# Retention stage of a two-block network on one core: state space steps over all head pairs, gate projection between token tiles, group norm and decays on GpSimd and ScalarE, one masked query product

## The chip, the cores and the metric

One core of a Trainium2 chip runs the whole program. The metric is device microseconds of one execution; the median of three runs before the change is 2362.76 us (2358.35 to 2370.51).

## The reference, cut to what matters

A first block (norm, input projection, retention beside a state space branch, mixing output, cross attention) is followed by a second one (two attentions and experts). The change touches retention and what shares its stage. All arrays have 1024 tokens; there are 8 heads with 64 columns for queries and keys and 128 for values, and chunks of 128 tokens:

```
proj = h @ w_in; q, k, v, g_ret, u, g_s5 = split(proj)
scores = einsum('bnihd,bnjhd->bnhij', qc, kc) * decay
inner  = einsum('bnhij,bnjhe->bnihe', scores, vc)
kv     = einsum('bnjhd,jh,bnjhe->bnhde', kc, k_w, vc)
R_next = chunk_decay * R + kv                    # a scan over the chunks
cross  = einsum('bnihd,ih,bnhde->bnihe', qc, q_w, R)
o   = (o - mean(o)) * rsqrt(var(o) + 1e-6)       # per head of 128 columns
ret = o * gn_g * silu(g_ret)
ssm = s5_branch(u) * silu(g_s5)
x   = x + concat([ret, ssm]) @ w_out
```

## The kernel before, in words

Products of float32 arrays run as three products of a high and a low part (`mm3`, lines 172 to 180). `weights` (L157) fetches a block of 1024 x 256 weights in two halves of 512 KB through one staging buffer `wraw`, casts each half to `whi` on ScalarE (L154) and subtracts on VectorE into `wlo` (L155); two such blocks fit at a time. All loads and stores named here are issued by SyncE, in one queue. The kernel writes instructions in program order, and a list scheduler then orders them for each engine: the earliest in program order that is ready goes first, so that later work fills gaps. On the chip each engine runs its own list strictly in order.

`retention` (L321) goes over four head pairs. For each pair it projects queries and keys of eight token tiles into the PSUM banks `m` (two of them), rotates them on VectorE (L356 to L360), and projects values (L367 to L371). Then comes a loop over four pairs of token tiles `m` (L437). `turn` (L377) transposes queries and keys of a tile on TensorE, copies the keys (`kT`, L384), multiplies the queries of each head by their decay into its half of a block-diagonal tile `qbd` (two VectorE instructions, L388) and once more into `qs` (L392), and scales the keys for the state (`kd`, two VectorE instructions, L397). `score` (L401) multiplies `kT` with `qbd` (L404) and `kd` with the values (L406), applies the mask (`st`, L408), and advances the state `rbd` with one VectorE instruction a head (L415, L417), since only its diagonal blocks hold anything. `output` (L420) multiplies `qs` with the state (256 columns, L422) and `st` with the values of each head (128 columns, L424). Between them `project` (L440) makes the retention gate. Group norm takes statistics of four heads (L463, L464), then an inverse root by a bit guess and two correction steps on VectorE (`rsqrt`, L182 to L198, tiles `rs_a` and `rs_y`), scales four times (L470) and multiplies by the gate (L472). `finish` (L426) transposes the result (L430) and stores it (L434, L435) in `ret_scr`; it is called one round later, as `late`.

`s5` (L594), the state space branch, is a generator of 32 steps: for each of 16 quads of groups, `phases` (angles, seven GpSimd instructions), `matrices` and `scan`, and for each two quads a `batch` that loads coefficients. `retention` yields the number of steps that are to be written next: two after every two token tiles of the query and value projections, none in the loop over `m`, so that in program order all 32 stand within the first two head pairs.

Behind retention, `mix_out` (L761) reads `ret_scr` back in eight blocks (`load_split`, L754: a load to `ls_raw`, which has two buffers, a cast to `r_hi`, a subtraction to `r_lo`; both tiles take memory that retention gives back). Next in program order is `h_last`, which is `s5_project` (L575) for the gate of the state space branch: four blocks of weights, each for four products of 24 matmuls of 512 columns, with a Silu on ScalarE (L588) and a 512 KB store for every two (L590). The first mixing product with `w_out` (L777 to L781) follows and reads all eight blocks of `ret` for every tile.

```
for steps in self.retention(h, rope, rc, rk, ret_scr):   # L1897
    for _ in range(steps):
        next(s5, None)
for _ in s5:
    pass
...
h2 = self.mix_out(hp, bp, lambda pj: self.s5_project(h, pj, g_scr, 4096, AF.Silu), ...)   # L1912
```

Of the kernel before, what the change touches and what calls it, by code (L numbers as in the profile page):

```python
# [20 lines left out]
P = 128  # L21
S = 1024
# [65 lines left out]
def lay_out(inputs):  # L88
    """The arrays of the launch: the inputs, those vectors that go along the partitions as columns, and the constants."""
# [30 lines left out]
class Net:  # L120
# [51 lines left out]
    def mm3(self, ps, lhs, rhs, ks, start=True, stop=True):  # L172
        """ps (+)= sum_k lhs_k^T rhs_k with both operands as exact float32r pairs; lhs, rhs: k -> (hi, lo)."""
# [39 lines left out]
    def normalise(self, xs, lo, n0):  # L213
        """Tiles xs [P tokens, D] in place to x / rms(x); the columns of the tiles from n0 in lo serve as scratch."""
# [9 lines left out]
    def gain(self, name):  # L224
        """A vector with features on the partitions, [P, k]."""
# [7 lines left out]
    def grow(self, name, pool, width=D):  # L233
        """A gain vector on every partition."""
# [6 lines left out]
    def to_feature(self, xs, hi, lo, n0, g):  # L241
        """Transpose the token tiles xs (each [P, D]) into columns n0*P.. of hi, lo [P, KD, tokens], times the gain g."""
# [11 lines left out]
    # ---------------------------------------------------------------- first norm  # L254
# [32 lines left out]
    def sincos(self, a, q, sin, cos):  # L287
        """sin and cos of the angles a, which (as q) is overwritten."""
# [10 lines left out]
    def exp_small(self, pool, x, name):  # L299
        """exp(x) to float32 accuracy on a small tile [p, n]."""  # L300
# [19 lines left out]
    # ---------------------------------------------------------------- retention  # L320
    def retention(self, h, rope, rc, rk, ret_scr):  # L321
        """Emits the retention branch, a step at a time."""
# [6 lines left out]
        qbd = [rc.tile([P, 2, P], F32, name=f"qbd{i}") for i in range(2)]  # L329
        rbd = [rc.tile([P, 2, P], F32, name=f"rbd{i}") for i in range(2)]  # L330
        for tl in qbd + rbd:
# [6 lines left out]
        for p in range(PAIRS):  # L338
            qw = rk.tile([P, P], F32, name="qw", tag="qw")
            nc.sync.dma_start(qw, t["k_ret_qw"][:, p * P:(p + 1) * P])  # L340
# [4 lines left out]
            for n in range(NT):  # L345
# [16 lines left out]
                if n % 2:  # L362
                    yield 2
            wv = self.weights([w[:, 1024 + p * 256:1024 + (p + 1) * 256]])
            vs = []
            for n in range(NT):
# [5 lines left out]
                if n % 2:  # L372
                    yield 2
# [3 lines left out]
            def turn(n):  # L377
                """Transposed queries (per head, with their decay) and keys of a token tile."""
# [6 lines left out]
                qb = qbd[n % 2]  # L385
                for h in range(2):
                    r = slice(h * 64, h * 64 + 64)
                    nc.vector.tensor_tensor(qb[r, h], ps[r, 0], qw[r], op=OP.mult)  # L388
                qs = None
                if n:  # L390
                    qs = rk.tile([P, P], F32, name="qs", tag="qs")
                    nc.vector.tensor_tensor(qs, ps[:, 0], qw, op=OP.mult)  # L392
                kd = None
                if n < NT - 1:
                    kd = rk.tile([P, 2, 64], F32, name="kd", tag="kd")
                    for h in range(2):
                        nc.vector.tensor_scalar(kd[:, h], qf[:, P + h * 64:P + h * 64 + 64], kw[:, 2 * p + h:2 * p + h + 1], None,  # L397
                                                op0=OP.mult)
                return kT, qb, qs, kd

            def score(n, kT, qb, kd):  # L401
                """Masked scores of a token tile and its term of the state."""
# [8 lines left out]
                Rn = rbd[n % 2]  # L411
                for h in range(2):
                    r = slice(h * 64, h * 64 + 64)
                    if n:
                        nc.vector.scalar_tensor_tensor(Rn[r, h], R[r, h], RET_G128[2 * p + h], ps[r, 1, h], op0=OP.mult, op1=OP.add)  # L415
                    else:
                        nc.vector.tensor_copy(Rn[r, h], ps[r, 1, h])  # L417
                return st, Rn

            def output(o, n, st, qs):  # L420
                if n:
                    nc.tensor.matmul(o, qs, R, start=True, stop=False)  # L422
                for h in range(2):
                    nc.tensor.matmul(o[:, h], st[:, h], vs[n][:, h], start=n == 0, stop=n == 0 or h == 1)  # L424

            def finish(p, m, on):  # L426
# [4 lines left out]
                rt = rk.tile([P, 2, 2 * P], F32, name="rt", tag="rt")  # L431
# [5 lines left out]
            for m in range(NT // 2):  # L437
# [12 lines left out]
                sa, Ra = score(n, a[0], a[1], a[3])  # L450
                if late:
                    late()
                output(o[:, 0], n, sa, a[2])
                R = Ra
                project(1)
                sb, Rb = score(n + 1, b[0], b[1], b[3])
                output(o[:, 1], n + 1, sb, b[2])
# [7 lines left out]
                var = rk.tile([P, 4], F32, name="gn_v", tag="gn_v")  # L465
                nc.vector.tensor_scalar(var, mv[:, :, 1], RS, RS * EPS, op0=OP.mult, op1=OP.add)
# [1485 lines left out]
```

## Time and profile before

| what | value |
|---|---|
| median of 3 runs | 2362.76 us (2358.35 to 2370.51) |
| span of the profiled execution | 2359.4 us (its time outside the span is not listed) |
| TensorE busy | 2115.9 us, 90% of the span |
| VectorE busy | 1367.9 us, 58% |
| ScalarE busy | 951.2 us, 40% |
| GpSimd busy | 553.9 us, 23% |
| mean granted TensorE clock | 0.937 |

Times in the profile count from the first instruction. The retention stage runs from about 175 us to 695 us, the mixing output follows. A granted clock of 1.00 is 2.4 GHz, one of 0.50 is 1.2 GHz. Engine columns give busy microseconds and, in brackets, the number of instructions.

### The profile page before, as it was taken

What the parts mean: (1) busy time and instruction counts of PE and PEld (TensorE: products, weight loads), DVE (VectorE), ACT (ScalarE), POOL (GpSimd) and SP (SyncE); (2) the same over time, 40 slices, a digit from 0 to 9 for tenths busy, and PEclk for the clock granted to TensorE, in tenths of its full rate; (3) what the DMA queues carried; (4) which work ended last, traced back from release to release, by engine and by line L of the source; (5) the groups of instructions that cost most, each with busy time, mean ns of one, the idle gap of its engine ahead of it and who ended that gap; (6) DMA issues with size and microseconds to landing.
All of it is one profiled execution on the core that took longest, in us unless ns stands there. A gap on an engine that the chain in (4) does not pass through costs nothing. (4 is left out here: it accounts for less than half of the span.)

```text
span 2359.4 us, 36272 instructions
## 1 busy us (share of the span) xinstructions
PE 2115.9 (90%) x13267; PEld 1886.6 (80%) x13267; DVE 1367.9 (58%) x3270; ACT 951.2 (40%) x1815; POOL 553.9 (23%) x625
## 2 busy tenths in 40 slices
PE   6998999998999999999998989899885888689991
PEld 5888898898988988988998979788764667667881
DVE  6508998999652335254525242646652557577775
ACT  5422433333334123044415343646743444256652
POOL 1024433344000002001003021224323643121115
PEclk9999999999999999999998999999876989789996
DMA  6642232222335533232122312243274773289985
GB/s 205 195 158 72 60 78 59 63 71 61 111 116 180 170 116 124 109 116 63 54 89 95 101 55 77 75 140 98 69 196 119 201 196 106 89 281 335 338 286 215
DMA packets 264746, 315.12 MB, mean 134 GB/s; under 512 B 38162, under 2 KB 218177, under 8 KB 264561
## 3 DMA queue, kind: packets, MB, share of 16 engines
q1 hardware_dynamic: 244048, 247.72, 33.9%
q0 software_dynamic: 11440, 40.36, 5.4%
q10 hardware_dynamic: 9072, 24.65, 2.7%
q8 instruction: 107, 1.75, 0.3%
q14 instruction: 79, 0.64, 0.1%
HBM read 228.02 MB, written 80.43 MB: 131 GB/s over the span
## 5 line engine op out<-in xcount | busy, mean ns | idle before, releaser
L155 DVE TENSOR_TENSOR wlo<-wraw,whi 128x1024 fp32r<-128x1024 f32 x220 | 273.6, 1249 | 286.1 <-ACT whi L154 285.2
L154 ACT CAST whi<-wraw 128x1024 fp32r<-128x1024 f32 x224 | 234.6, 1052 | 405.7 <-PE psm L180 174.1
L178 PE MATMUL psm<-whi,h_lo 128*128 128x256 f32 x768 | 226.4, 295 | 3.0 <-DVE ropeB L357 1.2
L179 PE MATMUL psm<-wlo,h_hi 128*128 128x256 f32 x768 | 223.4, 291 | 0.0
L180 PE MATMUL psm<-whi,h_hi 128*128 128x256 f32 x768 | 221.2, 288 | 0.0
L178 PEld LDWEIGHTS psm<-whi,h_lo 128*128 128x128 f32 x768 | 148.6, 193 | 6.2 <-issue 3.0
L179 PE MATMUL psm<-h_lo,whi 128*128 128x512 f32 x384 | 150.9, 393 | 0.0
L180 PE MATMUL psm<-h_hi,whi 128*128 128x512 f32 x384 | 150.2, 391 | 0.0
L180 PEld LDWEIGHTS psm<-whi,h_hi 128*128 128x128 f32 x768 | 148.5, 193 | 1.3 <-issue 0.8
L179 PEld LDWEIGHTS psm<-wlo,h_hi 128*128 128x128 f32 x768 | 148.6, 194 | 1.0 <-issue 0.2
L178 PE MATMUL psm<-h_hi,wlo 128*128 128x512 f32 x384 | 148.8, 392 | 0.0
L178 PE MATMUL psm<-hn_hi,wlo 128*128 128x512 f32 x256 | 103.8, 406 | 4.1 <-DVE dq L1093 3.8
L180 PE MATMUL psm<-hn_hi,whi 128*128 128x512 f32 x256 | 102.6, 401 | 0.0
L179 PE MATMUL psm<-hn_lo,whi 128*128 128x512 f32 x256 | 102.6, 401 | 0.0
L795 POOL TENSOR_TENSOR yr<-yr,sg 128x1024 f32<-128x1024 f32 x8 | 23.5, 2935 | 312.3 <-DMA yr<-y_scr 160.6
L830 DVE TENSOR_TENSOR res<-psm,res 128x256 f32<-128x256 f32 x64 | 27.1, 424 | 102.4 <-PE psm L180 100.5
L178 PEld LDWEIGHTS psm<-h_hi,wlo 128*128 128x128 f32 x384 | 72.1, 188 | 15.1 <-DVE qo_lo L155 0.2
L180 PEld LDWEIGHTS psm<-h_hi,whi 128*128 128x128 f32 x384 | 72.1, 188 | 14.6
L179 PEld LDWEIGHTS psm<-h_lo,whi 128*128 128x128 f32 x384 | 72.1, 188 | 14.3
L178 PE MATMUL psm<-whi,xl 128*128 128x512 f32 x184 | 77.1, 421 | 3.9 <-DVE xl L155 3.8
L178 PE MATMUL psm<-whi,hn_lo 128*128 128x256 f32 x256 | 75.6, 295 | 1.6 <-DVE hn_lo L251 1.4
L178 PE MATMUL psm<-whi,s_lo 128*128 128x256 f32 x256 | 72.8, 284 | 4.7 <-DVE res L830 3.9
(613 smaller groups left out, 6623.5 us busy)
## 6 DMA issues: line engine op xcount, KB each, us to landing
wraw<-w_in SPq DMA_DIRECT2D x40, 512.0 KB
wraw<-w_gate SPq DMA_DIRECT2D x64, 256.0 KB
wraw<-w_up SPq DMA_DIRECT2D x64, 256.0 KB
wraw<-w_down SPq DMA_DIRECT2D x32, 512.0 KB
wraw<-w_in SPq DMA_DIRECT2D x48, 256.0 KB
wraw<-w_out SPq DMA_DIRECT2D x24, 512.0 KB
y_all<-ye ACTq DMA_DIRECT2D x23, 512.0 KB
y_all<-zero POOLq DMA_DIRECT2D x13, 512.0 KB, 3.8
```

Source lines behind the costliest of these rows:

```text
L154: nc.scalar.copy(hi, src)
L155: (eng or nc.vector).tensor_tensor(lo, src, hi.bitcast(F32), op=OP.subtract)
L178: self.nc.tensor.matmul(ps, ll, rh, start=start and j == 0, stop=False)
L179: self.nc.tensor.matmul(ps, lh, rl, start=False, stop=False)
L180: self.nc.tensor.matmul(ps, lh, rh, start=False, stop=stop and j == n - 1)
L795: nc.gpsimd.tensor_tensor(yr, yr, sg, op=OP.mult)
L830: self.nc.vector.tensor_tensor(res[n][:, cs], ps, res[n][:, cs], op=OP.add)
```

## The change

- The 32 state space steps are spread: one instead of two after every two token tiles, so that they reach over all four head pairs.
- Three of the four weight blocks of the state space gate projection move from `mix_out` into the loop over `m`: a new generator `s5_gate` gives one product of 24 matmuls for each round, 12 in all. Its result tile `go` has one buffer and goes out in pieces of 64 elements. `mix_out` keeps the last block (`first=6`).
- Queries are multiplied once, by a table `qw` [128, 2, 128] that is zero where a head has no rows; the result `qb` serves the scores and, a head at a time, the product with the state, which is now 128 columns twice. The state keeps its off-diagonal blocks and advances with one instruction of 256 columns and a decay column `fall`.
- The key decay `kd` goes to GpSimd as one instruction. In the group norm the inverse root becomes two GpSimd instructions (an add of epsilon, a power of -0.5), the scaling four ScalarE activations with a scale and a bias `off`, and the multiplication by the gate goes to GpSimd. `rt` has one buffer.
- In `batch` the sign changes and copies of the coefficients `Cm` and `C` go from VectorE to ScalarE.

```diff
-        qbd = [rc.tile([P, 2, P], F32, name=f"qbd{i}") for i in range(2)]
-        rbd = [rc.tile([P, 2, P], F32, name=f"rbd{i}") for i in range(2)]
+        mhalf = rc.tile([P, 4], F32, name="mhalf")
+        nc.gpsimd.memset(mhalf, -0.5)
+        fall = rc.tile([P, PAIRS], F32, name="fall")
...
+        qws = [rc.tile([P, 2, P], F32, name=f"qw{i}") for i in range(2)]
...
-            qw = rk.tile([P, P], F32, name="qw", tag="qw")
-            nc.sync.dma_start(qw, t["k_ret_qw"][:, p * P:(p + 1) * P])
+            qw = qws[p % 2]
+            for j in range(2):
+                r = slice(64 * j, 64 * j + 64)
+                nc.sync.dma_start(qw[r, j], t["k_ret_qw"][r, p * P:(p + 1) * P])
...
-                    yield 2
+                    yield 1, 0
...
-                qb = qbd[n % 2]
-                for h in range(2):
-                    r = slice(h * 64, h * 64 + 64)
-                    nc.vector.tensor_tensor(qb[r, h], ps[r, 0], qw[r], op=OP.mult)
-                qs = None
-                if n:
-                    qs = rk.tile([P, P], F32, name="qs", tag="qs")
-                    nc.vector.tensor_tensor(qs, ps[:, 0], qw, op=OP.mult)
+                qb = rk.tile([P, 2, P], F32, name="qb", tag="qb")
+                nc.vector.tensor_tensor(qb, ps[:, 0][:, None, :].to_broadcast([P, 2, P]), qw, op=OP.mult)
...
-                    for h in range(2):
-                        nc.vector.tensor_scalar(kd[:, h], qf[:, P + h * 64:P + h * 64 + 64], kw[:, 2 * p + h:2 * p + h + 1], None,
-                                                op0=OP.mult)
+                    nc.gpsimd.tensor_tensor(kd, qf[:, P:].rearrange("p (h d) -> p h d", h=2),
+                                            kw[:, 2 * p:2 * p + 2, None].to_broadcast([P, 2, 64]), op=OP.mult)
...
+                Rn = rk.tile([P, 2, P], F32, name="R", tag="R")
+                if n:
+                    nc.vector.scalar_tensor_tensor(Rn, R, fall[:, p:p + 1], ps[:, 1], op0=OP.mult, op1=OP.add)
+                else:
+                    nc.vector.tensor_copy(Rn, ps[:, 1])
...
-                if n:
-                    nc.tensor.matmul(o, qs, R, start=True, stop=False)
                 for h in range(2):
-                    nc.tensor.matmul(o[:, h], st[:, h], vs[n][:, h], start=n == 0, stop=n == 0 or h == 1)
+                    if n:
+                        nc.tensor.matmul(o[:, h], qb[:, h], R[:, h], start=True, stop=False)
+                    nc.tensor.matmul(o[:, h], st[:, h], vs[n][:, h], start=n == 0, stop=True)
...
-                rs = self.rsqrt(var, 4)
+                nc.gpsimd.tensor_scalar(rs, mv[:, :, 1], 1.0, EPS, op0=OP.mult, op1=OP.add)
+                nc.gpsimd.tensor_tensor(rs, rs, mhalf, op=OP.pow)
+                off = rk.tile([P, 4], F32, name="gn_o", tag="gn_o")
+                nc.vector.scalar_tensor_tensor(off, mv[:, :, 0], -1.0, rs, op0=OP.mult, op1=OP.mult)
...
-                    nc.vector.tensor_scalar(on[:, i], of[:, i], mv[:, i, 0:1], rs[:, i:i + 1],
-                                            op0=OP.subtract, op1=OP.mult)
-                nc.vector.tensor_tensor(on, on, gate.rearrange("p j (h e) -> p (j h) e", h=2), op=OP.mult)
+                    nc.scalar.activation(on[:, i], of[:, i], AF.Identity, bias=off[:, i:i + 1], scale=rs[:, i:i + 1])
+                nc.gpsimd.tensor_tensor(on, on, gate.rearrange("p j (h e) -> p (j h) e", h=2), op=OP.mult)
...
-                yield 0
+                yield 0, 1
...
+    def s5_gate(self, h, tile, dst, b0):
...
+        ww = self.weights([self.t["w_in"][0][:, 4096 + b0 * P:4096 + (b0 + 2) * P]])
+        for b in (b0, b0 + 1):
+            for half in range(2):
+                ps, c, hs = self.bank("m"), (b - b0) * P, slice(half * 512, half * 512 + 512)
+                self.mm3(ps, lambda k: (ww[0][:, k, c:c + P], ww[1][:, k, c:c + P]), lambda k: (hh[:, k, hs], hl[:, k, hs]), range(KD))
+                o = tile()
+                nc.scalar.activation(o.rearrange("p j c -> p c j"), ps.rearrange("p (c j) -> p c j", j=S5_T), AF.Silu)
+                nc.sync.dma_start(dst[b].rearrange("p (j c) -> p j c", j=S5_T)[:, :, half * 64:half * 64 + 64], o)
+                yield
...
+            nc.scalar.mul(Cm[:, 1:3], Ci[:, None, :].to_broadcast([P, 2, N]), -1.0)
+            nc.scalar.mul(Cm[:, 3], Cm[:, 0], -1.0)
...
-            nc.vector.tensor_copy(C, ps)
+            nc.scalar.copy(C, ps)
...
+                    gate = (x for b0 in (0, 2, 4) for x in self.s5_gate(
+                        h, lambda: rk.tile([P, S5_T, 64], F32, name="go", tag="go", bufs=1), g_scr, b0))
+                    for steps, gates in self.retention(h, rope, rc, rk, ret_scr):
                         for _ in range(steps):
                             next(s5, None)
+                        for _ in range(gates):
+                            next(gate, None)
...
-            h2 = self.mix_out(hp, bp, lambda pj: self.s5_project(h, pj, g_scr, 4096, AF.Silu), y_scr, g_scr, ret_scr, x1_scr)
+            h2 = self.mix_out(hp, bp, lambda pj: self.s5_project(h, pj, g_scr, 4096, AF.Silu, first=6), y_scr, g_scr, ret_scr, x1_scr)
```

## Rows read from the trace of the kernel before

**Rows 1.** Busy time by stretch, all engines; after the busy columns the granted clock.

```profile
175.00:250.00 75.00, 68.80 (x548) 66.48 (x547) 59.33 (x133) 23.89 (x40) 34.33 (x22) 0.95 0.28 67
250.00:600.00 350.00, 325.06 (x2514) 309.73 (x2514) 328.08 (x895) 128.09 (x217) 138.70 (x90) 0.96 0.26 66
600.00:664.00 64.00, 62.82 (x505) 61.26 (x504) 37.42 (x128) 16.63 (x35) 0.00 (x0) 1.00 0.33 99
694.00:757.00 63.00, 63.00 (x286) 52.30 (x285) 15.84 (x13) 26.87 (x28) 2.39 (x1) 1.00 0.54 179
```

**Rows 2.** Waits of TensorE, 175 to 664 us: total us, times, longest us.

```profile
PE psa L422 <- DVE on L470: 4.6, 1, 4.6
PE pst L381 <- DVE qk L360: 4.1, 1, 4.1
PE pss L685 <- DVE rs_a L196: 4.0, 1, 4.0
PE psa L404 <- DVE on L470: 3.7, 3, 2.8
```

**Rows 3.** Busy time around one of these waits; the clock is the third number from the end.

```profile
283.00:288.00 5.00, 0.52 (x5) 0.32 (x3) 4.77 (x18) 3.56 (x4) 3.54 (x3) 0.97 0.25 50
288.00:295.00 7.00, 5.75 (x19) 4.38 (x20) 6.84 (x17) 2.67 (x6) 0.98 (x1) 0.54 0.10 25
```

**Rows 4.** Groups of VectorE instructions, 175 to 700 us: count, busy us, mean ns.

```profile
L470 DVE TENSOR_SCALAR on<-psa,gn_mv,rs_y 128x128 f32<-128x128 f32 x64 | 21.8, 403 | 0.4
L388 DVE TENSOR_TENSOR qbd<-pst,qw 64x128 f32<-64x128 f32 x64 | 18.2, 284 | 2.1 <-ACT kT L384 1.4
L397 DVE TENSOR_SCALAR kd<-qk,c_ret_kw 128x64 f32<-128x64 f32 x56 | 15.8, 321 | 0.6
L472 DVE TENSOR_TENSOR on<-on,gate 128x512 f32<-128x512 f32 x16 | 13.8, 863 | 1.7 <-issue 1.5
L415 DVE SCALAR_TENSOR_TENSOR rbd<-rbd,psa 64x128 f32<-64x128 f32 x48 | 13.4, 280 | 0.4
L408 DVE TENSOR_TENSOR st<-psa,mask 128x256 f32<-128x256 f32 x32 | 13.2, 412 | 12.2 <-PE psa L406 8.2 <-PE psa L404 3.9
```

**Rows 5.** VectorE instructions that touch `rs_a`, 175 to 700 us.

```profile
175.00:700.00 525.00, 35.79 (x160) 0.97 0.28 74
```

**Rows 6.** Instructions that touch `Cm`, 175 to 700 us: TensorE, weight loads, VectorE.

```profile
175.00:700.00 525.00, 3.31 (x16) 2.24 (x16) 11.88 (x32) 0.97 0.28 74
```

**Rows 7.** Groups of GpSimd instructions, the first at 175 to 700 us, the other at the end.

```profile
L660 POOL TENSOR_TENSOR ang<-ang,sn 128x512 f32<-128x512 f32 x16 | 23.5, 1470 | 1.3
...
L1843 POOL TENSOR_TENSOR r<-ss,mhalf 128x2 f32<-128x2 f32 x3 | 4.0, 1323 | 0.2
```

**Rows 8.** Timeline of VectorE: the same instruction at two times.

```profile
194.34 1.59 DVE L572 TENSOR_TENSOR Otmp<-C,s_Ai 128x576 f32<-128x576 f32 x1
...
288.63 0.75 DVE L572 TENSOR_TENSOR Otmp<-C,s_Ai 128x576 f32<-128x576 f32 x1
```

**Rows 9.** Busy time in these two stretches; the fifth engine column is GpSimd.

```profile
194.34:195.93 1.59, 1.35 (x12) 1.14 (x10) 1.59 (x3) 0.00 (x0) 1.51 (x2) 1.00 0.03 7
288.63:289.38 0.75, 0.69 (x2) 0.00 (x0) 0.75 (x3) 0.05 (x1) 0.00 (x0) 0.50 0.01 1
```

**Rows 10.** Groups of TensorE instructions, 664 to 693.5 us: the gate projection's first product.

```profile
L178 PE MATMUL psm<-h_hi,wlo 128*128 128x512 f32 x38 | 15.4, 404 | 0.0
```

**Rows 11.** Timelines of TensorE and VectorE at the end of retention.

```profile
682.36 0.60 PE L424 MATMUL psa<-v,st 128*128 128x128 f32 x4
693.48 0.60 PE L430 MATMUL pst<-c_ident,on 128*128 128x128 f32 x4
...
721.59 1.23 DVE L155 TENSOR_TENSOR r_lo<-ls_raw,r_hi 128x1024 fp32r<-128x1024 f32 x1 [2.22 <-ACT r_hi L154]
```

**Rows 12.** Waits of SyncE's queue, 175 to 700 us: total us, times, longest us.

```profile
SPq L167 <- DVE wlo L155: 48.7, 14, 9.1
```

More of the change, by code (lines that the diff above doesn't have):

```diff
@@ L328, in retention @@
         gng = self.gain("ret_gn_g")
-        qbd = [rc.tile([P, 2, P], F32, name=f"qbd{i}") for i in range(2)]
-        rbd = [rc.tile([P, 2, P], F32, name=f"rbd{i}") for i in range(2)]
-        for tl in qbd + rbd:
+        mhalf = rc.tile([P, 4], F32, name="mhalf")
+        nc.gpsimd.memset(mhalf, -0.5)
+        fall = rc.tile([P, PAIRS], F32, name="fall")
+        for p in range(PAIRS):
+            for j in range(2):
+                nc.gpsimd.memset(fall[64 * j:64 * j + 64, p:p + 1], RET_G128[2 * p + j])
+        qws = [rc.tile([P, 2, P], F32, name=f"qw{i}") for i in range(2)]
+        for tl in qws:
             nc.gpsimd.memset(tl, 0.0)
@@ L338, in retention @@
         for p in range(PAIRS):
-            qw = rk.tile([P, P], F32, name="qw", tag="qw")
-            nc.sync.dma_start(qw, t["k_ret_qw"][:, p * P:(p + 1) * P])
+            qw = qws[p % 2]
+            for j in range(2):
+                r = slice(64 * j, 64 * j + 64)
+                nc.sync.dma_start(qw[r, j], t["k_ret_qw"][r, p * P:(p + 1) * P])
             mask = rk.tile([P, 2, P], F32, name="mask", tag="mask")
@@ L372, in retention @@
                 if n % 2:
-                    yield 2
+                    yield 1, 0
             wg = self.weights([w[:, 2048 + p * 256:2048 + (p + 1) * 256]])
@@ L430, in finish @@
                         nc.tensor.transpose(ps[:, h, j], on[:, 2 * j + h], self.ident)
-                rt = rk.tile([P, 2, 2 * P], F32, name="rt", tag="rt")
+                rt = rk.tile([P, 2, 2 * P], F32, name="rt", tag="rt", bufs=1)
                 for h in range(2):
@@ L449, in retention @@
                 b = turn(n + 1)
-                sa, Ra = score(n, a[0], a[1], a[3])
+                sa, Ra = score(n, *a)
                 if late:
                     late()
-                output(o[:, 0], n, sa, a[2])
+                output(o[:, 0], n, sa, a[1])
                 R = Ra
                 project(1)
-                sb, Rb = score(n + 1, b[0], b[1], b[3])
-                output(o[:, 1], n + 1, sb, b[2])
+                sb, Rb = score(n + 1, *b)
+                output(o[:, 1], n + 1, sb, b[1])
                 R = Rb
@@ L573, in cmul, with s5_project @@
         e.tensor_tensor(o, o, tmp, op=OP.add if sign > 0 else OP.subtract)
-    def s5_project(self, h, pj, dst, base, func, then=None):
+    def s5_gate(self, h, tile, dst, b0):
         nc = self.nc
         hh, hl = h
-        for b0 in range(0, KD, 2):
+        ww = self.weights([self.t["w_in"][0][:, 4096 + b0 * P:4096 + (b0 + 2) * P]])
[7 more added lines that the diff above has]
+                yield
+    def s5_project(self, h, pj, dst, base, func, then=None, first=0):
+        nc = self.nc
+        hh, hl = h
+        for b0 in range(first, KD, 2):
             ww = self.weights([self.t["w_in"][0][:, base + b0 * P:base + (b0 + 2) * P]])
@@ L619, in batch @@
             nc.vector.tensor_scalar(By[:64], By[:64], -1.0, None, op0=OP.mult)
[L620 to L627 removed]
+            Cm = sk.tile([P, 4, N], F32, name="Cm", tag="Cm")
+            Ci = sk.tile([P, N], F32, name="Ci", tag="Ci")
+            for dst, src in ((Cm[:, 0], "s5_c_re"), (Ci, "s5_c_im")):
+                nc.sync.dma_start(dst, t[src][0, gs].rearrange("g p n -> (g p) n"))
+            nc.scalar.mul(Cm[:, 1:3], Ci[:, None, :].to_broadcast([P, 2, N]), -1.0)
+            nc.scalar.mul(Cm[:, 3], Cm[:, 0], -1.0)
             ps = self.bank("s", [P, 2, 8, p])
             for j in range(2):
[L630 removed]
+                nc.tensor.transpose(ps[:, j].rearrange("p g q -> p (g q)"), Cm[:, 2 * j:2 * j + 2].rearrange("p d n -> p (d n)"), self.ident)
             z["C"] = C = sk.tile([P, 2, 8, p], F32, name="C", tag="C")
[L632 removed]
+            nc.scalar.copy(C, ps)
             frb = fr[:, gs, None].to_broadcast([P, 8, p])
@@ L1896, in build @@
                     s5 = self.s5(tables, sk, u_scr, y_scr)
-                    for steps in self.retention(h, rope, rc, rk, ret_scr):
+                    gate = (x for b0 in (0, 2, 4) for x in self.s5_gate(
+                        h, lambda: rk.tile([P, S5_T, 64], F32, name="go", tag="go", bufs=1), g_scr, b0))
+                    for steps, gates in self.retention(h, rope, rc, rk, ret_scr):
                         for _ in range(steps):
                             next(s5, None)
+                        for _ in range(gates):
+                            next(gate, None)
                     for _ in s5:
```

24 lines of the change are left out of this document (4 added, 20 removed).

## Prediction

> **What bounds the kernel now.** I read the table of stretches first [rows 1]. Its first three rows are the stage that the change rewrites, up to the point where only the last head pair is left. From 250 to 600 us VectorE is busy for 328.08 of 350 us, that is 94%, and in the same stretch TensorE stands still for 350 - 325.06 = 24.9 us and has a granted clock of 0.96. From 600 to 664 us VectorE is down to 58%, and TensorE idles 1.2 of 64 us at a clock of 1.00. So TensorE is the engine with the most to do everywhere, and it loses time just where VectorE is full. The waits of TensorE name the same cause [rows 2]: the longest ones end with the scaling of the group norm (L470), the steps of its inverse root (L196) and the rotated queries (L360), all VectorE instructions in a queue that is never empty. The clock comes on top. A wait at 283 to 288 us leaves TensorE 0.52 us of work, and the seven microseconds behind it run at a granted clock of 0.54, the lower level of 1.2 GHz for nearly all of them [rows 3].
>
> What the stage loses, to 664 us: 6.2 + 24.9 + 1.2 = 32.3 us of standing still, and 5% of 75 us and 4% of 350 us for the clock, 17.8 us [rows 1]. Together **50 us**. That is the prize. The number of columns that TensorE multiplies is the same after the change, and the moved gate projection only changes its place.
>
> **The change part by part.** *VectorE loses work.* What goes or shrinks, in busy time: scaling 21.8, decayed queries 18.2, key decay 15.8, product with the gate 13.8, state 13.4 [rows 4], inverse root 35.8 [rows 5], coefficients 11.9 [rows 6]: 130.7 us. What comes: 32 query products of 256 columns out of PSUM and 28 steps of the state of the same shape, each like the mask's 412 ns [rows 4], so 13.2 + 11.5 us; 16 small instructions for the offset at 35.79 / 160 = 0.22 us, 3.6 us; and the subtractions of three weight blocks, six at the 1.23 us of a block of that shape [rows 11], 7.4 us. Net, VectorE goes from 424.8 us (175 to 664 us, rows 1) to about 330. The stage itself grows by the twelve gate products: 24 matmuls each at 63 / 286 = 0.22 us [rows 1], 63 us in all. 489 - 35 + 63 = 517 us, so VectorE would be at 64%, close to the 58% at which TensorE lost 1.2 of 64 us.
>
> *Spreading the state space steps* I cost at nothing by itself: VectorE is full until 600 us, long after the two head pairs within which all 32 steps stand in program order, so the steps already run late and far spread. What hides the moved order is the list order itself; without that cover, at worst the full loss of before stays, which is a bound on what VectorE's relief gives.
>
> *GpSimd and ScalarE gain work.* GpSimd gets 16 gate products at the 1.47 us of its 512-column instruction, 56 key decays of a quarter of that size (between a quarter of 1.47 us and all of it) and 16 powers. A power of two columns took 1.32 us [rows 7]; for four columns I take twice that, 2.6 us, between 1.3 and 5.3, and the addition ahead of it as no longer. It stood at 139 of 350 us [rows 1], so it has room. On the path this matters once a round: the inverse root took 160 / 16 = 10 instructions of 0.22 us, 2.2 us, and now takes 2.6 to 5.3 us or more before the scaling frees the PSUM bank for the next scores. Unhidden, 16 rounds would pay between 6 and 50 us; the cover is the gate product that each of the first twelve rounds gets, 24 x 0.22 = 5.3 us, and I take nothing for those rounds. ScalarE adds 64 scalings (at most the 403 ns they took on VectorE, 26 us) to 128 of 350 us; it stays under half.
>
> GpSimd's work has a second price. One and the same VectorE instruction took 1.59 us while GpSimd was busy for 1.51 of these 1.59 us, and 0.75 us with GpSimd at rest [rows 8, 9]. Some 90 us more of GpSimd, if VectorE ran at half speed through its share of them, would be 57 us more for VectorE, 75% of the stage. I count half of that, and keep both ends in the range. The Trainium skill, GPSIMD Engine Reference, section "8. Key points", says that GpSimd shares its SBUF interfaces with VectorE and contends with VectorE instructions that have two SBUF inputs; the trace agrees, as the instruction of rows 8 is one of those. By that rule taken to its end VectorE would stand at the 75%, and the stage would lose what rival C loses, 2364 us; by the rows at half of it, the sum below.
>
> *One masked query product* replaces 256 columns of state product by twice 128. The pair of 128-column products behind it takes 0.60 us [rows 11]; if each half cost as much as a whole, 28 x 0.6 = 17 us would come; I take 0, since the columns are the same. The extra `qw` load in each pair, six more stores, and the small memsets are issued long before anyone waits for them.
>
> *The gate projection leaves its place behind retention*, and this is where I see the largest cost. Before, the last transposes stand at 693.48 us, and the last of the eight blocks of `ret` that the mixing product needs is ready at 721.59 + 1.23 = 722.8 us [rows 11]: 29.3 us for the store, the loads through two buffers and the split. Nothing shows of it, since 63 us of gate projection run there without a gap [rows 1]. Three quarters of that are gone now. Also, the last head pair uses the projection as its filler: 38 of its triples, 38 x 3 x 0.22 = 25 us, ran before 693.5 us [rows 10]. In all that is 88 us, of which 22 stay. If the last pair still eats 25 us, nothing is left for the 29.3 us, and 3 us are missing besides. The two `m` banks let two token tiles take seven of eight blocks ahead, 2 x 7 x 3 x 0.11 = 4.6 us. That gives a hole of up to 28 us. If the last rounds need only 10 us of filler (last score product at 682.36, transposes 11 us later, rows 11), 12 us remain as cover and the hole is 13 us. I take 18 us, nearer to the middle as VectorE was not full there, and 3 us for the low clock after it, as behind the wait in rows 3.
>
> **The sum.** Left in the stage: 1.8% of 517 us, 10 us, and half of the start's 6.2 + 3.8 us, which the first quad's own load keeps: 15 us. The hole: 21 us. 50 - 15 - 21 = 14 us gained on a span of 2359.4, so 2345; the median of the runs stands 3.4 us above that span, which gives **2348 us**. With the bounds of the hole (13 to 31 with the clock) and 10 to 25 us left in the stage, this case reaches from 2335 to 2360.
>
> **Rivals.** *B, the hole does not open.* The last rounds, no longer behind a full VectorE, need little filler, or the projection's last block is kept for the end. Speaks for it: without the queue the norm ends sooner. Against: the list takes the earliest ready work, so filler goes first. 50 - 15 - 3 = 32 us gained: 2330 us.
>
> *C, the stage keeps waiting.* Only two weight blocks fit, and in the loop over `m` both are now in use, so the next pair's query weights can be split only after the last round. 29.3 us for eight blocks make 3.7 us for each 512 KB, 7.3 us for a weight block; less the last gate product's 5.3 us that is 2 us, and with the low clock 5.4, at three pair changes 16 us. (GpSimd's hold on VectorE would cost about as much.) Then 31 us stay in the stage: 2364 us, no change. Against: the list can fetch the first half into the staging buffer early.
>
> *D, slower.* The result tile `go` has one buffer, its store goes through SyncE's queue, and the next Silu waits for it at the head of ScalarE, with the key copies and the group norm's scaling behind. SyncE held its queue for weights 14 times, 3.5 us on average and up to 9.1 [rows 12]. A wait of 3.5 us that reaches TensorE costs 3.4 us of clock as well. It decides from four of the eleven reuses on, 4 x 6.9 = 28 us; with six it is 2348 + 41 = 2389 us. Against: reuses lie over 5 us of TensorE work apart.
>
> **How the numbers follow.** A 0.46, B 0.22, C 0.20, D 0.12. About 0.5% (12 us) is what a measurement of this kernel can tell from no change; the lines are 2351 and 2375 us. Of A 0.27 lies below 2351, with B and 0.01 of C that is 0.50. The rest of A, 0.15 of C and 0.02 of D make 0.36; 0.04 of C and 0.10 of D are slower, 0.14. The range, 2318 to 2378, takes in A, nearly all of B, and C with its bounds; it leaves out D and the far end of B.
>
> **What would show it.** Right: VectorE near 65% from 250 to 600 us, no wait of TensorE on the group norm over 2 us, few stretches at the low clock there; the last transposes some 20 to 30 us later than before, then a gap of TensorE on `r_lo` or `r_hi` of about 18 us. Wrong: no such gap (B); waits on `whi` or `wlo` at the pair changes (C); ScalarE's `go` waiting for its store, with TensorE waiting behind `kT` or `on` (D).

## The result, and the profile after

The changed kernel takes 2337.57 us (median of four runs, 2329.73 to 2341.98) where the kernel before took 2360.56 beside it. The ratio is 0.9889, interval 0.9849 to 0.9929: 23 us or 1.1% faster, 10 us below the forecast of 2348 and inside its range. The profiled execution has a span of 2327.9 us.

The table of stretches of the changed kernel (columns as in [rows 1]: busy TensorE, weight loads, VectorE, ScalarE, GpSimd, then granted clock):

```profile
175.00:250.00 75.00, 72.88 (x580) 69.69 (x579) 59.78 (x123) 28.33 (x51) 38.98 (x28) 1.00 0.31 75
250.00:600.00 350.00, 346.05 (x2602) 326.19 (x2600) 240.80 (x524) 145.08 (x271) 158.80 (x126) 1.00 0.30 77
600.00:664.00 64.00, 62.86 (x523) 61.48 (x524) 49.92 (x98) 27.74 (x49) 27.28 (x20) 1.00 0.24 64
694.00:717.00 23.00, 20.06 (x97) 16.44 (x95) 7.43 (x14) 12.20 (x16) 4.88 (x4) 1.00 0.67 230
717.00:738.00 21.00, 12.31 (x50) 10.96 (x51) 10.36 (x10) 7.31 (x7) 2.68 (x1) 0.51 0.70 235
```

From 250 to 600 us VectorE fell from 94% to 240.80 / 350 = 69%, TensorE's idle time from 24.9 to 4 us, and the clock rose from 0.96 to 1.00. The last two rows are the price: behind retention TensorE stands still for 2.9 and 8.7 us, and runs at 1.2 GHz for nearly all of the 21 us of the last row.

What TensorE waited for from 175 to 780 us (total us, times, longest):

```profile
PE psm L178 <- DVE r_lo L155: 11.2, 6, 3.5
PE pss L706 <- DVE W L573: 2.3, 5, 0.9
PE psm L178 <- DVE ropeB L364: 2.0, 2, 1.3
PE psm L178 <- ACT v L377: 1.5, 1, 1.5
```

The group norm, which led the list of [rows 2], is gone from it. In its place stands `r_lo`, the last step of reading retention's result back, in six waits.

Where the hole begins and ends, in TensorE's timeline (start, us, instruction, in brackets the idle time before it):

```profile
703.96 0.60 PE L429 MATMUL pst<-c_ident,on 128*128 128x128 f32 x4
...
711.02 0.39 PE L180 MATMUL psm<-h_hi,whi 128*128 128x512 f32 x1
711.25 0.28 PE L178 MATMUL psm<-whi,r_lo 128*128 128x256 f32 x1
...
715.83 0.39 PE L178 MATMUL psm<-whi,r_lo 128*128 128x256 f32 x1 [2.28 <-DVE r_lo L155]
...
722.94 0.58 PE L178 MATMUL psm<-whi,r_lo 128*128 128x256 f32 x1 [3.48 <-DVE r_lo L155]
...
732.29 0.58 PE L178 MATMUL psm<-whi,r_lo 128*128 128x256 f32 x1 [1.00 <-DVE r_lo L155]
```

And the end of the read-back in VectorE's timeline, which answers to the last of [rows 11]:

```profile
731.01 1.23 DVE L155 TENSOR_TENSOR r_lo<-ls_raw,r_hi 128x1024 fp32r<-128x1024 f32 x1 [1.43 <-ACT r_hi L154]
```

The last transposes come at 703.96 us, 10.5 us later than before, and the last block is split at 731.01 + 1.23 = 732.2 us. Of these 28.3 us the gate projection that was left covers 7.3 (to 711.25). Then the mixing products run in sixes, one block of `ret` for two token tiles, each behind a wait.

**Counting the losses.** The idle time alone doesn't tell all, as ends of matmuls are modelled. So I also counted each TensorE instruction at the median distance to the next one that its kind shows at full clock with no wait between them (0.23 us for 512 columns in the lines above), and took the sum from the length of the stretch. "Stage" is from the first product of the state space inputs to the last transposes of the group norm, "tail" from there to the products of the mixing stage's gated linear unit. The level of such a count depends on what is taken as a kind: by lines of the kernel the stage lost 59 us before and 16 to 17 after, by matrix sizes alone 76 and 30; the fall, 42 to 46 us, depends on it less. The third column is the length of stage and tail together, which needs no counting.

| kernel | stage: loss, of it idle | tail: loss, of it idle | stage and tail, us | VectorE 250 to 600 us | ratio to the kernel before, interval |
|---|---|---|---|---|---|
| before | 58.7, 32.3 | 0.2, - | 762.2 | 94% | 1 |
| after | 16.4, 7.2 | 18.4, 12.5 | 739.6 | 69% | 0.9889 [0.9849, 0.9929] |
| after, run again | 15.8, 6.6 | 19.6, 12.3 | 740.4 | 69% | 0.9880 [0.9863, 0.9898] |
| spread alone | 50.6, 29.3 | 0.4, - | 754.6 | 92% | 0.9964 [0.9945, 0.9982] |
| moves alone | 28.8, 15.0 | -0.2, - | 732.2 | 79% | 0.9890 [0.9865, 0.9915] |
| both, no gate block moved | 19.3, 7.4 | -0.3, - | 722.3 | 78% | 0.9839 [0.9817, 0.9861] |
| one gate block moved | 16.3, 6.7 | -0.1, - | 721.7 | 77% | 0.9836 [0.9819, 0.9854] |
| two gate blocks moved | 17.4, 7.6 | 5.5, 5.0 | 727.1 | 73% | 0.9858 [0.9836, 0.9881] |
| after, four buffers | 16.0, 7.0 | 11.2, 7.8 | 732.1 | 69% | 0.9844 [0.9823, 0.9865] |
| two blocks, four buffers | 21.4, 8.5 | 1.4, 2.5 | 726.8 | 72% | 0.9844 [0.9823, 0.9866] |
| no block moved, old group norm | 30.0, 14.0 | -1.0, - | 732.7 | 88% | 0.9867 [0.9849, 0.9885] |
| no block moved, old queries and state | 26.7, 12.5 | 1.1, - | 731.3 | 86% | 0.9875 [0.9859, 0.9890] |
| no block moved, coefficients on VectorE | 27.3, 12.7 | -0.9, - | 729.8 | 81% | 0.9838 [0.9822, 0.9854] |

Before to after: (58.7 + 0.2) - (16.4 + 18.4) = 24 us, which is the 23 us of the medians. The rest of the 31.5 us between the two spans is 3.6 us of an earlier start of the stage and some 5 us at the end, where nothing was changed.

Each profile is one execution. The changed kernel, run twice, took 739.6 and 740.4 us for stage and tail, but 1505.8 and 1516.1 us from there to the end. Over all thirteen profiles that last part, which no edit touches, takes 1505.8 to 1532.7 us. So medians of two variants that are a few us apart can't be told apart, and what an edit did is seen best in the lengths of stage and tail.

### The profile page after: what moved, and what is told of

Its sections match the earlier page's. It is cut to its first block, busy times and chain, and to the rows that moved or that the text cites. A ratio compares the mean times of both kernels' runs of the same rounds, so it can differ in the third digit from the quotient of the medians.

```text
span 2327.9 us, 36170 instructions
## 1 busy us (share of the span) xinstructions
PE 2094.9 (90%) x13323; PEld 1869.5 (80%) x13323; DVE 1286.5 (55%) x2846; ACT 980.3 (42%) x1904; POOL 615.8 (26%) x708
## 5 line engine op out<-in xcount | busy, mean ns | idle before, releaser
L178 PE MATMUL psm<-whi,r_lo 128*128 128x256 f32 x256 | 75.4, 294 | 12.5 <-DVE r_lo L155 11.2
```

The lines of the kernel that those rows point to most:

```text
L178: self.nc.tensor.matmul(ps, ll, rh, start=start and j == 0, stop=False)
```

## The experiments

Lines in the diffs are shortened to the part that changes. Every edit also gives the list scheduler other lists to order; what such a new order does by itself was not separated, so a few us between two variants can be its work.

**Spread alone.** The kernel before with only the state space steps spread (in both places where it yields):

```diff
-                    yield 2
+                    yield 1
```

> The kernel before, with one state space step instead of two after every two token tiles, and nothing else. Theory (the gain comes from VectorE's relief, the order of the steps does nothing): no change, within 6 us of the kernel before (2354 to 2366), VectorE still over 90% busy from 250 to 600 us and TensorE still losing 40 to 50 us there to standing still and the low clock. Rival (the spread is what relieves the stage): 25 us faster or more, VectorE well under 90%.

Measured 2356.5 us, ratio 0.9964 [0.9945, 0.9982], 8.5 us faster. From 250 to 600 us:

```profile
250.00:600.00 350.00, 327.35 (x2570) 313.68 (x2569) 321.89 (x892) 127.60 (x217) 128.57 (x84) 0.97 0.27 67
```

TensorE gained 2.3 us of busy time and 0.01 of clock over [rows 1], and VectorE is still 92% full. The order of the state space steps is worth something even with a full VectorE, less than the rival's 25 us and more than the theory's nothing.

**Moves alone.** The changed kernel with the steps as before and all gate blocks behind retention:

```diff
-                    yield 1, 0
+                    yield 2, 0
...
-                yield 0, 1
+                yield 0, 0
...
-self.s5_project(h, pj, g_scr, 4096, AF.Silu, first=6)
+self.s5_project(h, pj, g_scr, 4096, AF.Silu, first=0)
```

> The changed kernel with two state space steps at a time as before and the whole gate projection behind retention as before: only the moves of work off VectorE and the masked query product are left. Theory: the stage loses about 15 us where it lost 50 to 58, and no hole opens behind it, so about 40 us faster than before (2315 to 2328). Rival (the gate products between token tiles are what fill TensorE's waits): less than 10 us faster than before, with waits of TensorE in the loop over the token tiles.

Measured 2342.14 us, ratio 0.9890 [0.9865, 0.9915]: 26 us, less than the 40 us expected and more than the rival's 10.

```profile
250.00:600.00 350.00, 337.63 (x2750) 326.59 (x2748) 275.49 (x601) 154.33 (x292) 182.82 (x140) 1.00 0.29 77
```

VectorE is down to 79%, but TensorE still idles 12.4 us of the 350.

**Both, no gate block moved.** The changed kernel with the last two lines of the diff above, and the steps spread.

> The changed kernel with the whole gate projection behind retention as before; the spread steps and the moves off VectorE stay. Theory: no hole before the mixing product, the clock at 1.00 there, and the 16 to 20 us that the hole and its low clock cost come back: 2316 to 2326, the same as the run with the moves alone. Rival (the gate products in the loop are needed as filler): waits of TensorE in the loop take the place of the hole, 2337 or slower.

Measured 2331.01 us, ratio 0.9839 [0.9817, 0.9861]. The time lies between the two ranges; there is no hole, as the theory said, and no waits in the loop like the rival's, but it is not the same as the run with the moves alone.

```profile
250.00:600.00 350.00, 344.47 (x2818) 334.81 (x2816) 274.00 (x609) 158.16 (x304) 180.18 (x144) 1.00 0.27 70
```

VectorE does the same work in the same 350 us as with the moves alone, and TensorE idles 5.5 us in place of 12.4. So the spread is worth about 38 - 26 = 12 us here (10 by the lengths of stage and tail); alone it was 8.5. And the kernel is about 11 us faster than the whole change (0.9839 against 0.9889 and 0.9880; 17 us by the lengths): moving the three gate blocks costs time.

**One gate block moved, two gate blocks moved.**

```diff
-gate = (x for b0 in (0, 2, 4) for x in self.s5_gate(
+gate = (x for b0 in (0,) for x in self.s5_gate(
...
-self.s5_project(h, pj, g_scr, 4096, AF.Silu, first=6)
+self.s5_project(h, pj, g_scr, 4096, AF.Silu, first=2)
```

(for two blocks `(0, 2)` and `first=4`.)

> The changed kernel with one of the four blocks of the gate projection in the loop over the token tiles (during the first head pair) and three behind retention. Theory: 65 us of projection behind it cover the last rounds' 25 us and the 29 us of loading, so no hole: 2316 to 2326. Rival (each block that leaves costs the same share): a third of the hole, 6 to 7 us, is there: 2324 to 2332.

> The changed kernel with two of the four blocks of the gate projection in the loop over the token tiles (first two head pairs) and two behind retention. Theory: 43 us of projection behind it, of which the last rounds use 15 to 25 us, leave 18 to 28 us against the 29 us of reading back: a rest of the hole of 0 to 8 us, 1.3 to 1.6% faster than before. Rival (the placing of the gate products costs by itself, in proportion): two thirds of the loss of 12 us, about 1.3% faster, with waits inside the loop.

One block: 2327.96 us, 0.9836 [0.9819, 0.9854], and no loss in the tail; the time alone fits the rival's range, the missing hole the theory. Two: 2327.93 us against another 2364.84, 0.9858 [0.9836, 0.9881], with 5.5 us lost in the tail, inside the theory's 0 to 8; three lose 18.4 to 19.6. The loss in the tail begins with the second block and grows with the third, and the stage is hardly better for it: it loses 19.3, 16.3, 17.4 and 16.4 us with none, one, two and three blocks moved. So the blocks bring at most 3 us where they went, no more than the count can tell.

With two blocks the read-back reaches TensorE by another way than with three. TensorE's waits from 690 to 760 us:

```profile
PE psm L178 <- ACT proj L602: 2.7, 1, 2.7
...
PE psm L178 <- DVE r_lo L155: 0.4, 1, 0.4
```

and ScalarE's instructions before that longest wait ends:

```profile
713.87 1.04 ACT L154 CAST r_hi<-ls_raw 128x1024 fp32r<-128x1024 f32 x1 [2.54 <-DMA ls_raw<-ret_scr]
714.82 1.06 ACT L602 ACTIVATE proj<-psm 128x512 f32<-128x512 f32 x1
```

The last gate product ends at 710.1 us. The activation `proj`, which frees its PSUM bank, stands on ScalarE behind the cast of the last block of `ret`, and that cast waits 2.54 us for its load. TensorE waits for the loads in both cases, but only 0.4 us of it shows under `r_lo` here.

**The result read back through four buffers.** `ls_raw` has two buffers; every second block goes to the tiles of another tag, which has two and is needed only later.

```diff
-            raw = pool.tile([P, S], F32, name="ls_raw", tag="ls_raw")
+            raw = pool.tile([P, S], F32, name="ls_raw", tag=tags[k % len(tags)])
...
-            self.load_split(wk, ret, [ret_scr[:, k] for k in range(KD)])
+            self.load_split(wk, ret, [ret_scr[:, k] for k in range(KD)], ("ls_raw", "sg"))
```

> The changed kernel whole, but the eight blocks of the retention result are read back through four buffers instead of two (every second one uses the buffers of the gate's rows, which are idle then). Theory (the hole is the time of reading back with nothing to cover it): the blocks come closer together, the last one some 6 us earlier, the hole and its low clock shrink by 6 to 10 us: 1.4 to 1.6% faster than before. Rival (the hole is set by the last rounds of retention and not by the reading): the same as the changed kernel, 1.1% faster than before.

Measured 2324.36 us, 0.9844 [0.9823, 0.9865]; the changed kernel beside it, on the same chip:

> The changed kernel once more, as it is, beside the three others on the same chip. Both theories: 1.0 to 1.2% faster than before, the hole before the mixing product 10 to 12 us with some 20 us of low clock.

2337.34 us, 0.9880 [0.9863, 0.9898]. TensorE's waits from 690 to 760 us, first with two buffers:

```profile
PE psm L178 <- DVE r_lo L155: 11.2, 6, 4.3
```

and with four:

```profile
PE psm L178 <- DVE r_lo L155: 4.9, 3, 3.1
```

The blocks' instructions on VectorE (shortest, median, longest ns; first and last start), with two buffers:

```profile
L155 DVE TENSOR_TENSOR r_lo<-ls_raw,r_hi x8: 1218/1224/1912, 706.9 to 730.5; 128x1024 fp32r<-128x1024 f32 x8
```

and with four:

```profile
L155 DVE TENSOR_TENSOR r_lo<-ls_raw,r_hi x8: 1215/1222/1226, 706.8 to 720.7; 128x1024 fp32r<-128x1024 f32 x8
```

The eight splits start over 13.9 us instead of 23.6, half the waits are gone, and of 23.9 us at the low clock 6.8 are left. The time is the theory's. That is the hole's mechanism shown: the loads through two buffers set the end of the read-back, and with it some 8 us of the loss. The other 11 us of the tail stay.

**Two gate blocks moved, four buffers.**

> Two gate blocks moved instead of three, and the result read back through four buffers instead of two. With three blocks moved the four buffers took 8 us off the 20 us that the hole costs; with two moved the hole costs 5.5 us, so here it should cost between 0 and 2 us, and the whole kernel 0.982 to 0.985 of the kernel before, 2 to 6 us below the kernel with two moved alone. Rival: the hole is set by the last split and not by the loads; then 4 to 6 us stay and the ratio is that of two blocks moved, 0.9858.

2329.05 us, 0.9844 [0.9823, 0.9866]. The tail loses 1.4 us, as expected, but the stage lost 4 us more in this profile than with two blocks alone, and in time the two (0.9844 and 0.9858) can't be told apart.

**The old group norm on VectorE**, with no gate block moved:

```diff
-                nc.gpsimd.tensor_scalar(rs, mv[:, :, 1], 1.0, EPS, op0=OP.mult, op1=OP.add)
-                nc.gpsimd.tensor_tensor(rs, rs, mhalf, op=OP.pow)
...
+                rs = self.rsqrt(var, 4)
...
+                    nc.vector.tensor_scalar(on[:, i], of[:, i], mv[:, i, 0:1], rs[:, i:i + 1],
+                                            op0=OP.subtract, op1=OP.mult)
+                nc.vector.tensor_tensor(on, on, gate.rearrange("p j (h e) -> p (j h) e", h=2), op=OP.mult)
```

> The run with the gate projection behind retention, but with the group norm's inverse root, scaling and gate product back on VectorE as before; spread steps, one query product, key decay and coefficients stay changed. Theory (VectorE's load is what holds TensorE, and the norm is over half of what was taken off it, some 70 of 130 us): VectorE back near 90% from 250 to 600 us, 15 to 25 us slower than that run, so 0.7 to 1.0% faster than before instead of 1.6%. Rival (the path through GpSimd and ScalarE counts, not the load: a longer chain in the norm costs as much as the load gives): within 5 us of that run, 1.4 to 1.8% faster than before.

2331.99 us, 0.9867 [0.9849, 0.9885]. VectorE is at 307.83 of 350 us:

```profile
250.00:600.00 350.00, 337.87 (x2728) 325.92 (x2726) 307.83 (x774) 136.26 (x245) 139.56 (x105) 0.99 0.28 68
```

and TensorE waits for the scaling again:

```profile
PE psa L404 <- DVE on L469: 5.0, 3, 2.5
```

About 7 us slower than the base (the kernel with both and no gate block moved) by the ratios, whose intervals overlap, and 10 to 11 us by the lengths and the count of losses. That is between the theory's 15 to 25 us and the rival's 5.

**The old queries, key decay and state**, with no gate block moved: the lines of `turn`, `score` and `output` of the kernel before, with its `qbd`, `qs` and `rbd`.

> The kernel with all four gate blocks behind retention (0.984 of the kernel before, VectorE 274 of 350 us between 250 and 600 us), with the old queries, key decay and state back on VectorE (two products a head and one for the state's queries, two key decays, two steps of the state with a head each). That gives VectorE back about 18 + 16 + 13 - 13 - 12 = 22 us of the stage, some 16 us of the 350: 290 us, 83%. Theory (what counts is how full VectorE is): between 78% at no cost and 88% at 7 to 11 us lies 3 to 6 us, a ratio of 0.985 to 0.987 to the kernel before. Rival (what counts is only the group norm's chain, from the statistics to the scaling that frees the bank): no more than 1 us, 0.983 to 0.985, with TensorE's waits as in the kernel with four blocks behind. A second rival, in which two products of 128 columns cost more than one of 256, makes this kernel faster: 0.976 to 0.982.

2335.78 us, 0.9875 [0.9859, 0.9890], about 8 us slower than the base and just past the slow end of what the first theory gave.

```profile
250.00:600.00 350.00, 340.25 (x2717) 326.78 (x2716) 301.40 (x713) 155.30 (x296) 166.46 (x123) 1.00 0.27 70
```

VectorE came to 86%, not 83%. From the last statistics of a round to the end of its scaling the median of 16 rounds is 5.1 us here and 4.6 us in the base, against 8.0 us with the old norm; so the group norm was nearly as fast here as in the base, and yet the kernel lost as much as with the old norm. The chain of the norm isn't special: work given back to VectorE elsewhere costs about the same. The old query products lie on TensorE's path too, though, so load and path are not fully separated. The second rival, that two products of 128 columns cost more than one of 256, can't be read from this time, as the run gives VectorE its work back as well. The traces settle it: from the start of a state product to the next start the median is 0.216 us for one of 256 columns (L422 of the kernel before) and 0.111 us for one of 128 (L422 of the changed kernel), so the new form costs 0.006 us more a pair, 0.3 us in all.

**The coefficients on VectorE**, with no gate block moved: `nc.scalar.mul` and `nc.scalar.copy` of `batch` as VectorE instructions.

> The same base, with only the sign changes and the copy of the coefficients back on VectorE: about 12 us more for VectorE in the stage, some 8 of the 350 us, 81%. Both theories: within 3 us of the base (0.983 to 0.986). If instead the copy of the coefficients out of PSUM stood in a full VectorE queue on the way to the state space products, as the bank waits of the kernel before would allow, 5 to 8 us slower: 0.986 to 0.988.

2327.07 us, 0.9838 [0.9822, 0.9854]: no difference to the base in time, at 81% of VectorE. The intervals leave room for some 6 us, and this run's profile does lose more in the stage, 27.3 us against 19.3: a single wait of 4.3 us on the rotated queries and keys (`qk`) that ends at 196 us, with the clock at 0.91 around it, is the largest part. Whether that comes from the coefficients or from this one execution isn't shown.

## Why the prediction was right, and where it was off

**The cause and the direction were right.** TensorE lost its time to a full VectorE, and the loss falls with VectorE's share: 58.7 us at 94%, 50.6 at 92%, 27 to 30 at 81 to 88%, 16 to 21 from 69 to 78%. (The moves alone lose 28.8 at 79%, so the placing matters as well as the share.) With the steps spread, the time shows no difference between 72 and 81%.

**The time came out 10 us below the forecast, mostly because the stage kept less than the sum left it.** The sum took 50 us of idle time and low clock as the prize, left 15 in the stage and gave 21 to the hole. In the same measure, the first three rows of the two tables of stretches, the changed kernel keeps 2.1 + 4.0 + 1.1 = 7.2 us at a clock of 1.00. The start keeps 2.1 us in place of 5, as the clock doesn't fall there, and the rest 5.1 us in place of 10. These 7.8 us and the 2.6 us by which the hole was smaller than 21 make the 10 us. Counted by spacing the stage's loss fell from 58.7 to 16.4 us, the same 42 us as from 50 to 7.2: the count sees some 9 us more than idle time and clock in both kernels, and 8 to 13 us more in all the others, so these 9 us were no part of the prize.

**"Spreading the state space steps I cost at nothing" failed.** The reason given holds: in the kernel before the scans of the steps start from 226 to 615 us, over all four head pairs already, and with the spread alone from 226 to 636 us. But it doesn't follow that the spread is free: it was worth 8.5 us alone and about 12 with the moves. How so small a shift earns that much stays open. It raised no term of the sum, because the sum took the whole prize less 15 us without asking which edit earns it; the moves alone would have left about 17 us of idle time and low clock in the stage, 28.8 by the count.

**VectorE's share** was foreseen at 64%, 69% with half of GpSimd's hold, over 517 us; over 175 to 692 us it is 363 / 517 = 70%. That is partly luck. The list of what goes leaves out `qs`, the variance `gn_v` and the copy of `C`, 15 us together in the kernel before, while the instructions that both kernels have in the same number grew by 21 us in sum, where half the hold was put at 28. Two slips changed nothing: the key decays are 28 instructions and not 56, and with both bad bounds, 25 us left and a hole of 31, the sum reaches 2369 us and not 2360. The prices of the parts, groups of instructions of the changed kernel from 175 to 760 us:

```profile
L472 POOL TENSOR_TENSOR on<-on,gate 128x512 f32<-128x512 f32 x16 | 20.7, 1295 | 26.9 <-ACT on L471 26.9
L466 POOL TENSOR_TENSOR gn_r<-gn_r,mhalf 128x4 f32<-128x4 f32 x16 | 17.4, 1087 | 1.2
L397 POOL TENSOR_TENSOR kd<-qk,c_ret_kw 128x128 f32<-128x128 f32 x28 | 14.9, 531 | 35.0 <-PE psa L406 28.0 <-DVE qk L367 6.9
L465 POOL TENSOR_SCALAR gn_r<-gn_mv 128x4 f32<-128x4 f32 x16 | 4.6, 287 | 104.7 <-DVE gn_mv L463 104.7
...
L471 ACT ACTIVATE on<-psa,gn_o,gn_r 128x128 f32<-128x128 f32 x64 | 24.2, 457 | 20.5 <-DVE gn_o L468 20.5
...
L408 DVE TENSOR_TENSOR st<-psa,mask 128x256 f32<-128x256 f32 x32 | 13.3, 416 | 18.5 <-PE psa L406 16.1 <-PE psa L404 2.2
L413 DVE SCALAR_TENSOR_TENSOR R<-R,fall,psa 128x256 f32<-128x256 f32 x24 | 11.2, 468 | 0.0
L468 DVE SCALAR_TENSOR_TENSOR gn_o<-gn_mv,gn_r 128x4 f32<-128x4 f32 x16 | 3.8, 239 | 9.8 <-POOL gn_r L466 9.8
...
L393 DVE TENSOR_TENSOR qb<-pst,qw 128x256 f32<-128x256 f32 x32 | 12.9, 411 | 15.6 <-ACT kT L391 15.5
```

The power of four columns took 1.09 us, below even the low bound of 1.3, and the addition 0.29. With the offset that is 1.6 us a round, less than the ten small instructions that it replaces (2.2 us). From the last statistics of a round to the end of its scaling the median fell from 9.5 to 3.4 us, so the 6 to 50 us of the unhidden rounds never had to be hidden. The key decay took 0.53 us (0.37 to 1.47 taken), the gate product 1.30 (1.47 taken). ScalarE's scaling took 457 ns, over the 403 that were called the most. The state took 0.47 us (0.41 taken) and the query product 0.41, as taken.

**GpSimd's hold on VectorE** is real, and it is selective. VectorE's groups from 250 to 600 us of the kernel before:

```profile
L356 DVE TENSOR_TENSOR ropeA<-psm,rope_cos 128x256 f32<-128x256 f32 x24 | 9.9, 414 | 1.4 <-PE psm L180 1.3
...
L360 DVE TENSOR_TENSOR qk<-ropeA,ropeB 128x128 f32<-128x128 f32 x24 | 9.6, 398 | 0.0
...
L573 DVE TENSOR_TENSOR W<-W,Otmp 128x512 f32<-128x512 f32 x13 | 8.9, 682 | 0.1
```

and of the changed one:

```profile
L366 DVE TENSOR_TENSOR qk<-ropeA,ropeB 128x128 f32<-128x128 f32 x21 | 11.0, 523 | 0.1
...
L573 DVE TENSOR_TENSOR W<-W,Otmp 128x512 f32<-128x512 f32 x10 | 9.9, 992 | 0.2
...
L363 DVE TENSOR_TENSOR ropeA<-psm,rope_cos 128x256 f32<-128x256 f32 x21 | 8.6, 411 | 0.5 <-PE psm L180 0.5
```

Instructions with one input in PSUM kept their price (414 and 411 ns; the mask's 412 and 416), while these two with both inputs in SBUF went from 398 to 523 and from 682 to 992 ns. Single executions of the changed kernel show it without the other changes: `qk` (L366) took 280 ns on average in the 17 with GpSimd at rest and 767 ns in the 10 with GpSimd busy throughout; `ropeA` took 411 and 410 ns. Not every instruction with two SBUF inputs paid: `W<-Ba,s_Ar` (128x512) took 678 ns before and 676 after. The Trainium skill, GPSIMD Engine Reference, section "8. Key points", names VectorE instructions with two SBUF inputs among those that contend with GpSimd; the trace agrees for `qk`, by its single executions. The full price, 75% of VectorE, didn't come, and at 69% little of it reached TensorE: it waited 2.3 us for `W`.

**The hole opened, by the mechanism named and near the size named.** The steps of the sum: last transposes to last block 28.3 us (29.3 taken); filler that the last head pair ate 22 - 7.3 = 14.7 us (between 10 and 25); idle 12.5 us (18 taken); clock 18.4 - 12.5 = 5.9 us (3 taken), because the low clock stayed for 20.5 us and not for some seven. In all 18.4 for 21, with a smaller wait and a longer low clock that offset each other in part. Two things turned out otherwise: the transposes came 10.5 us later than before, not 20 to 30, and there is no single gap of 18 us but six waits of up to 3.5 us, since each block that arrives releases six products.

**The rivals.** B (no hole, 2330 us) didn't happen in the changed kernel; it is what happens with no block or one block moved, 2331.01 and 2327.96 us. C's waits on `whi` and `wlo` at the pair changes don't appear in the list of waits. D's price did not come up: the twelve `go` activations took 1.10 us each, and no engine waited for one; SyncE held its queue for the weight blocks as before (49.6 us in 14 waits; 48.7 us in [rows 12]), and no wait of TensorE in the stage ends with a load or with `go`.

**The best version.** One gate block moved (0.9836), none moved (0.9839), two or three moved with four buffers (0.9844 each) are all about 1.6% faster than the kernel before and some 10 us faster than the changed one; among themselves they can't be told apart. More buffers for `go`, or four for `ls_raw` under its own tag, were not tried.

## What to carry to other kernels

With the busiest engine's feeder at 90% and more, relief paid steeply here until it was near 80% and its work spread evenly; below that no run shows a gain in time. Of the groups put back here, the group norm and the queries cost about the same, so it mattered little which instructions were moved; move those that are cheap elsewhere. Filler work that covers a store and a read-back must not be moved ahead of it before the read-back is counted (here 28 us against 7 us of cover); moving a part of it, or reading back through more buffers, keeps the gain. When two ways of counting a loss disagree, take both before and after: here they differ by 9 us in both kernels, and only the difference between kernels is a gain. And where an edit touches one part of a program, compare that part: the rest, unchanged, scattered by 27 us between profiles.

## What the runs showed of the hardware

- TensorE at the low level of its clock stayed there while it worked in runs of six products with waits of 1 to 3.5 us between them: 20.5 us at 0.50 from 717.4 to 737.9 us. Its last wait ended at 732.29 us; it worked on without a wait, and the clock rose to 1.00 at 737.9 us. With half of the waits gone the low clock lasted 6.8 us. Here the low clock cost about half as much again as the waits themselves (5.9 us on 12.5).
- One VectorE instruction with two SBUF inputs (`qk`, 128x128) took 280 ns with GpSimd at rest and 767 ns with GpSimd busy throughout; one with an input in PSUM (`ropeA`, 128x256) took 411 and 410 ns.
- GpSimd's power is not priced by the column here: four columns took 1.09 us, two took 1.32 at another place [rows 7].
